# A hybrid recurrent, attention and expert layer: merging the branches with an accumulating DMA

## The chip, the cores and the metric

The kernel runs on one core of a Trainium2 chip. The core has five engines with queues of their own: TensorE (PE in the profile; PEld is its weight load), VectorE (DVE), ScalarE (ACT), GpSimd (POOL) and SyncE (SP). Each works through its instructions in order and waits where an instruction's input or buffer is not there. DMA transfers are issued from SP's queue or from GpSimd's. The metric is the time of one execution on the device, in microseconds (us); lower is better.

## The reference, cut to what matters

One layer over 1024 latent tokens of 1024 channels, with 256 context tokens ahead of them. A recurrent branch (`rnn`) and an attention branch (`attn`) are computed, merged with two sigmoid gates, projected, and added to the input; then a routed mixture of 16 experts follows. The change lies in the merge:

```python
def merge_branches(rnn, attn, zg, p):
    g = jax.nn.sigmoid(zg).reshape(B, L, N_BRANCH, D_MODEL)
    merged = g[:, :, 0] * (rnn @ p['w_rnn_out']) + g[:, :, 1] * (attn @ p['w_mla_out'])
    return merged @ p['w_o']

x_new = x + mod_l[2] * merge_branches(rnn_l, attn_l, z_l[5], p)
x_new = x_new + mod_l[5] * ec_moe(modulate(rmsnorm(x_new, p['g_norm2']), mod_l[3], mod_l[4]), p)
```

The experts can only begin when every token has been routed, and routing needs `x_new` of all tokens.

## The kernel before

All matrix products are made from pairs of values: `split` (lines 93 to 95) makes a high part by a cast on ACT and a low part by a subtraction on DVE, and `mm3` (lines 97 to 100) adds three products. The stages run one after the other: projections, recurrent branch, its output projection, attention, merge and output projection, routing, experts.

The first summand of the merge is finished early. Lines 858 to 869 multiply the recurrent branch's product by its gate and store it to `s0_d` in DRAM, as 8 blocks of 128 channels by 1024 tokens. The second gate lies in `s1_d` in the same form.

The merge is the stage opened at line 1007. It has two halves of 512 tokens (`hf`), each with 8 blocks of 128 channels (`b`). `mo_mm(hf, b)` makes the product of the attention branch with `w_mla_out`, 12 matmuls into one of three PSUM banks. `mo_out(hf, b)` (lines 1034 to 1042) loads `a0` (the finished first summand) and `s1` (the second gate), 256 KB each, from SP's queue; multiplies the product in PSUM by `s1` on DVE (line 1040), which frees the bank; adds `a0` on DVE (line 1041); and splits the sum into `mh` and `ml`. When the 8 blocks of a half are issued, `xo(ph, t)` multiplies them by `w_o`: 4 token tiles by two column halves, 24 matmuls each, which read `mh` and `ml` block by block (`k`) and pairs of split weights `woh`, `wol` (`load_wo`). In the first half the first three blocks are run over three quarters of the contraction before the last quarter, since the attention's last normalisation (lines 931 to 935: DVE, GpSimd, ACT, DVE for each of 8 slices) is still under way.

The order of the matmuls is written out by hand (`manual_schedule` over PE). On the other engines, and on SP's queue, a planner puts the instructions in order before the run from its own costs, so an instruction can stand ahead of one that the program names earlier; on the chip each queue then keeps that order. A tile of which `bufs` copies exist can be written again when the readers of the copy from `bufs` turns ago are done; both `a0` and `s1` have four copies.

Of the kernel before, what the change touches and what calls it, by code (L numbers as in the profile page):

```python
# [19 lines left out]
F32 = mybir.dt.float32  # L20
# [4 lines left out]
OP = mybir.AluOpType  # L25
AX = mybir.AxisListType

P = 128
D = 1024
KD = D // P  # L30
# [30 lines left out]
def layer_kernel(ctx: ExitStack, tc: tile.TileContext, I, rope_tab, out, dbg=None):  # L61
    nc = tc.nc
# [30 lines left out]
    def split(h, l, src):  # L93
        nc.scalar.copy(h, src)  # L94
        nc.vector.tensor_tensor(l, src, h.bitcast(F32), OP.subtract)  # L95
# [26 lines left out]
    s0_d = dram.tile([KD, P, SEQ], F32, name="s0_d")  # L122
# [771 lines left out]
    p6a = p6ac.__enter__()  # L894
# [114 lines left out]
    with pool("p6b", side="right") as p6b, pool("p6", side="right") as p6:  # L1009
# [11 lines left out]
        mw, mp, wo = {}, {}, {}  # L1021
# [11 lines left out]

        def mo_out(hf, b):
            ts = slice(hf * 512, (hf + 1) * 512)
            a0 = p6a.tile([P, 512], F32, name="a0", bufs=4)
            nc.sync.dma_start(a0, s0_d[b][:, ts])
            s1 = p6a.tile([P, 512], F32, name="s1", bufs=4)
            nc.sync.dma_start(s1, s1_d[b][:, ts])
            nc.vector.tensor_tensor(s1, mp.pop((hf, b)), s1, OP.mult)  # L1040
            nc.vector.tensor_tensor(s1, s1, a0, OP.add)
            split(mh[:, b], ml[:, b], s1)

        wraw = {}
# [84 lines left out]
        with tc.manual_schedule(engines={mybir.EngineType.PE}):  # L1129
            for hf in range(2):  # L1130
                if hf == 0:
                    for ks in (range(3), range(3, 4)):
                        for b in range(3):
                            mo_mm(0, b, ks)
                            if ks[0]:
                                mo_out(0, b)
# [3 lines left out]
                    for b in range(3, KD):  # L1140
                        mo_mm(0, b)
                        mo_out(0, b)
                        if b >= 4:
                            load_wo(0, b - 4)
                    nc.vector.scalar_tensor_tensor(bc[2], bc[2], 1.0, g2b, op0=OP.add, op1=OP.mult)
                else:
                    mh, ml = merged()
                    for b in range(KD):
                        mo_mm(1, b)
                        if b < 2:  # L1150
                            tail[0][b]()
                            if b == 1:
                                tail.pop()
                        mo_out(1, b)
# [213 lines left out]
```

## Time and profile before

| | us |
|---|---|
| median of 3 executions (lowest, highest) | 1769.93 (1767.58, 1776.2) |
| the profiled execution, its own time | 1771.81 |
| its span in the trace | 1769.8 |
| PE busy | 1687.1 (95%) |
| DVE busy | 1313.4 (74%) |
| ACT busy | 1014.9 (57%) |
| POOL busy | 264.5 (15%) |
| first half's blocks of the merge, first to last `mo` matmul | 988.75 to 1016.81 |
| second half's blocks | 1073.39 to 1096.52 |

A timeline row gives the start, the duration, the engine, the line, the operation, the tile written and the tiles read; in brackets stands how long the engine had been idle and what released it. Matmuls overlap, so a row of 0.39 us can be followed by the next 0.23 us later. In these views the digits of a tile's name are left out: `a` is `a0` and `s` is `s1` in the merge stage.

### The profile page before, as it was taken

Reading aid. Unit: us, or ns where it says so; the run is one execution under the profiler, and the core shown is the slowest. Engines: PE = TensorE matmul, PEld = TensorE weight load, DVE = VectorE, ACT = ScalarE, POOL = GpSimd, SP = SyncE. Lnnn points to the kernel's source line nnn. Section 1 sums busy time; section 2 is a strip of 40 time slices with the busy share of each in tenths; the row PEclk is TensorE's granted clock in tenths of the full one; section 3 lists DMA queues with packets and bytes.
Section 4 is the critical chain, followed back from the end, with each engine's and each line's share of the span. In section 5 each row is a group of like instructions: output and inputs, shape, how many; then the busy total and the mean of one; then the engine's idle time right before and its main releaser. Section 6 shows DMA issues by size and latency. Waiting matters only on the chain.

```text
span 1769.8 us, 20838 instructions
## 1 busy us (share of the span) xinstructions
PE 1687.1 (95%) x7823; PEld 1356.9 (77%) x7823; DVE 1313.4 (74%) x1607; ACT 1014.9 (57%) x1105; POOL 264.5 (15%) x196
## 2 busy tenths in 40 slices
PE   8999999999999999999999999939999999999996
PEld 3788887888887877777777678827888888888885
DVE  4755456788886454787877657587999999989996
ACT  2533324876788313667776532316777777777773
POOL 1123331211221100111210100020121111112101
PEclk9999999999999999999999999969999999999999
DMA  8264444435443934000000355667999999999981
GB/s 328 100 181 101 108 121 140 131 126 167 155 144 117 318 136 152 28 28 28 29 1 1 138 199 213 234 261 286 379 395 391 403 399 381 399 402 380 389 309 24
DMA packets 174179, 363.72 MB, mean 206 GB/s; under 512 B 40160, under 2 KB 90744, under 8 KB 174080
## 3 DMA queue, kind: packets, MB, share of 16 engines
q1 hardware_dynamic: 168896, 343.54, 53.6%
q0 software_dynamic: 5184, 18.88, 4.0%
q8 instruction: 61, 1.00, 0.2%
q14 instruction: 38, 0.31, 0.0%
HBM read 314.84 MB, written 47.54 MB: 205 GB/s over the span
## 4 chain that ended last, share of the span: by engine, by line
PE 71%; DVE 11%; ACT 6%; issue 4%; DMA 4%; POOL 3%; SPq 0%; POOLq 0%; DVEq 0%; ACTq 0%
PE w_e_gate L99 3%; PE w_e_gate L100 3%; PE w_e_gate L98 3%; PE w_e_down L99 3%; PE w_e_down L100 3%; PE w_e_down L98 3%; PE w_e_up L99 3%; PE w_e_up L98 3%; PE w_e_up L100 3%; PE z L99 2%; PE z L98 2%; PE z L100 2%; PE pm L816 2%; POOL st L143 2%; PE s L98 2%
## 5 line engine op out<-in xcount | busy, mean ns | idle before, releaser
L95 DVE TENSOR_TENSOR el<-ma,eh 128x2048 fp32r<-128x2048 f32 x114 | 258.2, 2286 | 22.2 <-PE w_e_down L99 10.8
L94 ACT CAST eh<-ma 128x2048 fp32r<-128x2048 f32 x114 | 217.9, 1917 | 73.7 <-PE w_e_up L100 28.7
L95 DVE TENSOR_TENSOR el<-me,eh 128x2048 fp32r<-128x2048 f32 x78 | 176.9, 2287 | 16.6 <-ACT eh L94 6.0
L94 ACT CAST eh<-me 128x2048 fp32r<-128x2048 f32 x78 | 149.0, 1916 | 47.4 <-PE w_e_gate L100 17.3
L906 ACT ACTIVATE pr<-s 128x512 f32<-128x512 f32 x160 | 95.8, 599 | 77.2 <-PE s L100 75.8
L818 DVE TENSOR_REDUCE mx<-pm 128x1 f32<-128x320 f32 x256 | 114.4, 483 | 22.8 <-PE pm L816 20.6
L99 PE MATMUL z<-xl,wh 128*128 128x512 f32 x320 | 125.2, 392 | 1.9 <-DVE xl L280 1.9
L98 PE MATMUL z<-xh,wh 128*128 128x512 f32 x320 | 125.2, 393 | 1.0 <-DVE xh L279 0.8
L100 PE MATMUL z<-xh,wl 128*128 128x512 f32 x320 | 125.0, 391 | 1.2 <-POOL wl L326 1.2
L1312 POOL DMA_INDIRECT out_dram<-y,icol x16 | 52.3, 3268 | 469.9 <-DVE y L1311 469.9
L94 ACT CAST wh<-wr 128x1024 fp32r<-128x1024 f32 (+1 forms) x53 | 52.0, 980 | 116.1 <-PE z L99 55.0
L95 DVE TENSOR_TENSOR pl<-pr,ph 128x1024 fp32r<-128x1024 f32 x64 | 81.0, 1265 | 31.4 <-ACT ph L94 24.7
L99 PE MATMUL w_e_up<-el,xgh 128*128 128x512 f32 x256 | 100.7, 394 | 0.6 <-DVE el L95 0.6
L98 PE MATMUL w_e_gate<-eh,xgh 128*128 128x512 f32 x256 | 101.1, 395 | 0.2 <-ACT xgh L94 0.2
L99 PE MATMUL w_e_gate<-el,xgh 128*128 128x512 f32 x256 | 101.2, 395 | 0.0
L100 PE MATMUL w_e_gate<-eh,xgl 128*128 128x512 f32 x256 | 100.1, 391 | 0.8 <-DVE xgl L95 0.8
L98 PE MATMUL w_e_down<-eh,hdh 128*128 128x512 f32 x256 | 99.7, 389 | 1.1 <-ACT hdh L94 1.1
L98 PE MATMUL w_e_up<-eh,xgh 128*128 128x512 f32 x256 | 100.7, 393 | 0.0
L99 PE MATMUL w_e_down<-el,hdh 128*128 128x512 f32 x256 | 100.6, 393 | 0.0
L100 PE MATMUL w_e_down<-eh,hdl 128*128 128x512 f32 x256 | 99.9, 390 | 0.5 <-DVE hdl L95 0.5
L100 PE MATMUL w_e_up<-eh,xgl 128*128 128x512 f32 x256 | 99.8, 390 | 0.0
L816 PE MATMUL pm<-kh,qh 97*128 97x320 f32 x256 | 86.6, 353 | 7.0 <-DVE kl L95 4.1
(349 smaller groups left out, 4368.7 us busy)
## 6 DMA issues: line engine op xcount, KB each, us to landing
ma<-in_w_e_down_dram SPq DMA_DIRECT2D x40, 1024.0 KB, 9.4
ma<-in_w_e_up_dram SPq DMA_DIRECT2D x38, 1024.0 KB, 8.0
ma<-in_w_e_gate_dram SPq DMA_DIRECT2D x36, 1024.0 KB, 7.2
me<-in_w_e_gate_dram SPq DMA_DIRECT2D x28, 1024.0 KB, 7.0
me<-in_w_e_up_dram SPq DMA_DIRECT2D x26, 1024.0 KB, 8.2
me<-in_w_e_down_dram SPq DMA_DIRECT2D x24, 1024.0 KB, 9.8
wr<-in_w_in_dram SPq DMA_DIRECT2D x32, 512.0 KB, 4.5
wr<-in_w_ada_dram SPq DMA_DIRECT2D x32, 512.0 KB, 4.2
```

Source lines behind the costliest of these rows:

```text
L94: nc.scalar.copy(h, src)
L95: nc.vector.tensor_tensor(l, src, h.bitcast(F32), OP.subtract)
L98: nc.tensor.matmul(o, lh, rh, start=start, stop=False)
L99: nc.tensor.matmul(o, lh, rl, start=False, stop=False)
L100: nc.tensor.matmul(o, ll, rh, start=False, stop=stop)
L143: nc.gpsimd.tensor_tensor(ap, ap, h, OP.pow)
L816: nc.tensor.matmul(pm[:, 0:320], qh[:, t * P:(t + 1) * P], kh[:, g * 320:(g + 1) * 320], start=True, stop=True)
L818: nc.vector.tensor_reduce(mx[:, g, t:t + 1], pm[:, 0:320], axis=AX.X, op=OP.max)
L906: nc.scalar.activation(pr[:, sl], sp_, AF.Exp)
L1312: nc.gpsimd.indirect_dma_start(out=out_rows, out_offset=bass.IndirectOffsetOnAxis(ap=icol[:, e:e + 1], axis=0), in_=y, in_offset=None, com ...
```

## The change

In blocks 0 to 5 of a half the addition on DVE goes. `s1` holds the gated attention product, and a DMA issued from GpSimd reads the first summand from DRAM and adds it into `s1` in place. The split of such a block is put into the program two blocks later (`late`). Blocks 6 and 7 keep the load of `a0` and the addition; ahead of block 6's multiplication the program splits what is still waiting (blocks 4 and 5). `s1` has six copies instead of four and `a0` two instead of four.

```diff
         def mo_out(hf, b):
             ts = slice(hf * 512, (hf + 1) * 512)
-            a0 = p6a.tile([P, 512], F32, name="a0", bufs=4)
-            nc.sync.dma_start(a0, s0_d[b][:, ts])
-            s1 = p6a.tile([P, 512], F32, name="s1", bufs=4)
+            s1 = p6a.tile([P, 512], F32, name="s1", bufs=6)
             nc.sync.dma_start(s1, s1_d[b][:, ts])
-            nc.vector.tensor_tensor(s1, mp.pop((hf, b)), s1, OP.mult)
-            nc.vector.tensor_tensor(s1, s1, a0, OP.add)
+            if b < KD - 2:
+
+                nc.vector.tensor_tensor(s1, mp.pop((hf, b)), s1, OP.mult)
+                nc.gpsimd.dma_start(out=s1, in_=s0_d[b][:, ts], accum_op=OP.add)
+                late.append((b, s1))
+            else:
+                a0 = p6a.tile([P, 512], F32, name="a0", bufs=2)
+                nc.sync.dma_start(a0, s0_d[b][:, ts])
+                while late:
+                    mo_split(*late.pop(0))
+                nc.vector.tensor_tensor(s1, mp.pop((hf, b)), s1, OP.mult)
+                nc.vector.tensor_tensor(s1, s1, a0, OP.add)
+                mo_split(b, s1)
+            if len(late) > 2:
+                mo_split(*late.pop(0))
+
+        late = []
+
+        def mo_split(b, s1):
             split(mh[:, b], ml[:, b], s1)
```

## Rows read from the trace of the kernel before

**Rows 1.** Page, part 4: the chain that ended last, shares by engine

```profile
PE 71%; DVE 11%; ACT 6%; issue 4%; DMA 4%; POOL 3%; SPq 0%; POOLq 0%; DVEq 0%; ACTq 0%
```

**Rows 2.** By stretches: length, busy PE, PEld, DVE, ACT, POOL, granted clock, DMA share, GB/s

```profile
997.00:1017.00 20.00, 16.86 (x61) 13.31 (x61) 17.41 (x26) 6.80 (x11) 1.51 (x1) 0.83 0.81 292
...
1001.00:1005.60 4.60, 4.60 (x12) 3.54 (x12) 3.98 (x7) 0.97 (x2) 0.00 (x0) 0.50 0.88 327
...
1073.00:1101.00 28.00, 28.00 (x132) 23.33 (x132) 21.55 (x40) 7.92 (x16) 0.55 (x1) 1.00 0.58 197
```

**Rows 3.** Timeline of PE in the first half of the merge stage

```profile
996.68 0.39 PE L100 MATMUL mo<-ath,wl 128*128 128x512 f32 x1
...
1000.15 0.80 PE L98 MATMUL mo<-ath,wh 128*128 128x512 f32 x1 [3.08 <-DVE s L1040]
...
1005.87 0.49 PE L99 MATMUL mo<-atl,wh 128*128 128x512 f32 x1
...
1017.04 0.39 PE L98 MATMUL xo<-woh,mh 128*128 128x512 f32 x1
...
1022.99 0.50 PE L99 MATMUL xo<-wol,mh 128*128 128x512 f32 x1 [1.28 <-DVE wol L95]
...
1024.97 0.50 PE L100 MATMUL xo<-woh,ml 128*128 128x512 f32 x1
```

**Rows 4.** Timeline of DVE, first half of the merge stage

```profile
997.32 1.21 DVE L95 TENSOR_TENSOR wol<-wr,woh 128x1024 fp32r<-128x1024 f32 x1
...
999.42 0.68 DVE L1040 TENSOR_TENSOR s<-mo,s 128x512 f32<-128x512 f32 x1
...
1013.45 0.68 DVE L1040 TENSOR_TENSOR s<-mo,s 128x512 f32<-128x512 f32 x1
...
1017.58 1.28 DVE L1041 TENSOR_TENSOR s<-s,a 128x512 f32<-128x512 f32 x2
...
1021.12 0.68 DVE L1040 TENSOR_TENSOR s<-mo,s 128x512 f32<-128x512 f32 x1
...
1021.73 1.21 DVE L95 TENSOR_TENSOR wol<-wr,woh 128x1024 fp32r<-128x1024 f32 x1
```

**Rows 5.** Timelines of DVE and PE, second half of the merge stage

```profile
1091.97 0.68 DVE L1040 TENSOR_TENSOR s<-mo,s 128x512 f32<-128x512 f32 x1
...
1096.75 0.39 PE L98 MATMUL xo<-woh,mh 128*128 128x512 f32 x1
...
1097.38 0.68 DVE L1040 TENSOR_TENSOR s<-mo,s 128x512 f32<-128x512 f32 x1
...
1099.48 0.69 DVE L95 TENSOR_TENSOR ml<-s,mh 128x512 fp32r<-128x512 f32 x1 [0.69 <-ACT mh L94]
...
1101.96 0.39 PE L100 MATMUL xo<-woh,ml 128*128 128x512 f32 x1
```

**Rows 6.** Instructions of tile mh: smallest, median, largest ns; first and last start

```profile
L94 ACT CAST mh<-s x16: 614/620/626, 1002.0 to 1098.8; 128x512 fp32r<-128x512 f32 x16
```

**Rows 7.** DMA issues: tiles, queue, count, KB, median us from issue to landing

```profile
s<-s_d SPq DMA_DIRECT2D x4, 256.0 KB, 3.8
...
xg<-h_d,icol POOLq DMA_INDIRECT x2, 4.5
...
rn_d<-ge POOLq DMA_DIRECT2D x1, 512.0 KB, 3.0
...
s_d<-sg POOLq DMA_DIRECT2D x3, 512.0 KB, 6.1
...
out_dram<-y,icol POOLq DMA_INDIRECT x16, 11.6
```

**Rows 8.** GpSimd beside VectorE: two timeline rows, and line 934 (smallest, median, largest ns)

```profile
577.53 3.49 DVE L95 TENSOR_TENSOR rl<-wr,rh 128x1024 fp32r<-128x1024 f32 x3
...
578.49 0.53 POOL L619 DMA_DIRECT2D s_d<-sg  x1
...
L934 POOL TENSOR_TENSOR num<-num,den x32: 448/462/1507, 765.5 to 997.3; 128x128 f32<-128x128 f32 x32
```

## The prediction

> **What bounds the kernel now.** I read the profile from the outside in: the chain of waits, then the merge stage by stretches, then that stage's timelines engine by engine, and last the DMA issues. The chain is 71% TensorE and 11% VectorE [rows 1], so time is won only where TensorE waits or runs slowly. In the stretch 997 to 1017 us, which holds most of the first half's blocks, DVE is busy 17.41 us of 20.00 and the granted clock averages 0.83; in the second half's stretch TensorE is busy 28.00 us of 28.00 and DVE 21.55 [rows 2]. So the reader is to see two halves with different limits.
>
> In the first half TensorE loses time in two places. After the 996.68 matmul it stands until 1000.15, because the three product banks are full until the first multiplication frees one; the cadence would have given 996.91, so 3.24 us go [rows 3]. Then it runs at the lower of its two clock levels (granted 0.50, 1.2 GHz) [rows 2]: 13 matmuls take 1000.15 to 1005.87, 5.72 us, where the full clock's cadence gives 13 x 0.2265 = 2.94; 2.78 us go. The cadence is that of the second half's first output tile, whose 24 matmuls start from 1096.75 to 1101.96, 23 steps in 5.21 us [rows 5]. The second place is the first half's first output tile: it starts at 1017.04 and its last matmul at 1024.97, where 5.21 us would give 1022.25 [rows 3]. That is 2.72 us, lost to DVE: the wait at 1022.99 is for a `w_o` split that DVE only began at 1021.73, right behind the last block's multiplication at 1021.12 [rows 3, 4]. The second half's first output tile has no such loss [rows 5].
>
> **The change part by part.** Twelve additions go, six in each half. A pair of them takes 1.28 us and a single such operation 0.68, so each costs the queue 0.60 us: 3.6 us of DVE per half [rows 4]. In the second half nothing waits for them: the last low part ends at 1099.48 + 0.69 = 1100.17, and the matmul that reads it first starts at 1101.96, a margin of 1.79 us [rows 5]. That part is worth nothing there.
>
> In the first half they stand in the queue that ends late. Two things move. First, `s1` of blocks 4 and 5 now has a copy of its own and is loaded ahead of the stage, and so is the `a0` of blocks 6 and 7. Block 4's multiplication ran at 1013.45 [rows 4]. In the second half the last multiplication started 0.63 us after the first output matmul (1097.38 against 1096.75) [rows 5]; put back by three blocks of 12 x 0.2265 = 2.72 us from 1017.04, block 4's could run at 1017.04 + 0.63 - 8.16 = 1009.5, block 5's at 1012.2, 6's at 1015.0, 7's at 1017.7. Second, what DVE still has to do from block 5's multiplication on: three multiplications, two additions and four splits, 9 x 0.60 = 5.4 us, and four operations on 1024 columns (three weight splits and one gain), each some 1.15 us of queue (1.21 less an overlap of about 0.06, an estimate from the 1.28 pair [rows 4]), 4.6 us. From 1012.2 that ends at 1022.2 if DVE never stands, and 1022.25 is what TensorE needs. I grant it 1 us of standing, about what the wait of 0.69 for a cast would make once or twice [rows 5]. So the first output tile loses about 1.0 us instead of 2.72: **a gain of 1.7 us**.
>
> What is added: twelve accumulating DMAs of 256 KB from GpSimd. No such DMA into SBUF is in the trace, so its time L from issue to landing is bounded by neighbours: a plain load of the same 256 KB lands in 3.8 us in this very stretch, plain stores of 512 KB from GpSimd's queue in 3.0 and 6.1, a gather of 512 KB into SBUF in 4.5, and the only accumulating ones, 512 KB scatters in the saturated expert stage, in 11.6 [rows 7]. I take L = 4.5, the row nearest in queue and direction, at twice the size, which makes up for the addition; the ends 3.0 and 11.6 stay for the range.
>
> The new wait is the cast `mh` on ACT, which now waits for a landing instead of a DVE addition; the weight casts queue behind it on ACT, and the low part and all later DVE work behind that cast. The cover is the delay of two blocks, 5.44 us. A block's multiplication (0.68), hand-over (0.1, estimate), landing (4.5) and cast (0.62 [rows 6]) take 5.9 us, so the low part comes just behind the multiplication two blocks on, and that one can be up to two blocks late before a bank is missed. Blocks 0 to 3 therefore cost nothing, even with L some 4 us longer. ACT, busy 6.80 us of 20.00, and GpSimd, 1.51 of 20.00 [rows 2], have room for waits and for twelve issues of about 0.53 us [rows 8]. On SP's queue twelve loads go. The load of block 6's `s1` now waits for block 0's split: 999.42 + 0.68 + 0.1 + 4.5 + 0.62 + 0.68 = 1006.0; with 3.8 to land it is there by 1009.8, and it is needed at 1015.0 (L = 11.6 would make it 2 us late).
>
> Block 5 is where the latency can show. First half: its multiplication ends at 1012.9, its sum lands at 1017.5, is cast by 1018.1, and its first reader, 15 steps into the output tile, is at 1020.4: covered. Second half: it ends at 1091.97 + 0.68 = 1092.65, the sum lands at 1097.25, is cast by 1097.9 and split by 1098.6; needed at 1096.75 + 15 x 0.2265 = 1100.15: covered. But in program order blocks 6 and 7 come behind that split: two multiplications, two additions and two splits from 1098.6, 6 x 0.60 = 3.6 us, the last low part done at 1102.3 where 1101.96 is needed, 0.4 us late; with the planner's order putting block 6 ahead, nothing. **I take a loss of 0.2 us.**
>
> One rule weighed. The trace has GpSimd's product of line 934 at 0.46 us in the median and 1.51 at the worst, and the worst is the one at 997.3, beside a DVE split of two SBUF operands [rows 4, 8]. But an issue from GpSimd's queue in the middle of three such splits took 0.53 us [rows 8]. The Trainium skill, page "SBUF — State Buffer", section "Who interferes with whom", says that a VectorE instruction with two SBUF inputs holds up a GpSimd instruction that reads SBUF, and only infers that descriptor generation is spared. The 0.53 us bears out the inference. By the rule without it each issue would take some 1.05 us more, and L would be 5.55: the second half's loss becomes about 1.2, and the gain of the whole falls to some 0.5 us.
>
> **The sum.** 1.7 - 0.2 = 1.5 us less. The profiled execution took 1771.81 us, 2.0 of it outside its span of 1769.8, and would take 1770.3; it lies 1.9 above the median of the three, so for the median I forecast 1769.93 - 1.5 = **1768.4 us**.
>
> **The rivals.**
> *Latency shows (slower).* The place is block 5 at the end of each half. The point is L = about 6: from there each further us costs both halves, some 2 us in all. At L = 8 block 5's cast in the second half ends at 1101.4, 1.25 us late, and the six DVE operations behind it leave the last low part about 2 us later still: 3.2 us there, and 3.2 instead of 2.72 in the first half, together 3.7 slower, 1773.6. At 11.6 both halves stop for about 4.9 us and trail 2 more, 6.9 + 6.9 - 2.7 = 11.1, and each stop, longer than the 3.24 us after which the clock fell [rows 2, 3], would bring the 2.78 us of slow matmuls again: 16.6 slower, 1786.5. For it: the only accumulating rows land in 11.6. Against: those scatters move twice the bytes, in a stage where expert weights fill the DMA engines; here the DMA share is 0.81 and 0.58 [rows 2].
>
> *The first stop goes too (faster).* If the planner's new order puts the first multiplication ahead of the `w_o` split at 997.32 and the normalisation's last piece, the 3.24 and 2.78 us go as well, and with all of the 2.72: 8.7 us, 1761.2. For it: that multiplication's product is complete by about 995, yet it ran at 999.42 [rows 4]. Against: what stands ahead of it is not touched by the change.
>
> *No effect.* The planner leaves the late `w_o` split where it is, the freed DVE time is idle, and the time stays at 1769.9. For it: the wait at 1022.99 is for that split, not for a sum [rows 3].
>
> **How the numbers follow.** Chances: forecast 0.52, with a range of its own of 1766 to 1771.5; no effect 0.12; latency 0.24, half of it beyond 8.85 us; first stop gone 0.12, two thirds of it, with some noise, beyond 8.85 us. A measurement of this kernel tells about 0.5%, 8.85 us, from no change. Faster by more than that: 0.08; slower: 0.12; within: 0.80. The range 1761 to 1779 leaves out half of the latency case and a little of the fastest.
>
> **What would show it.** Right: no additions on DVE for blocks 0 to 5; block 4's multiplication near 1009.5; accumulating DMAs landing in 3.8 to 6 us; the first half's first output tile spread over about 6 us instead of 7.9, the second's over 5.2 to 5.6. Wrong: a TensorE wait released by `mh` of block 5 in either half, a second stretch at clock 0.50, GpSimd issues far above 0.53 us, or a first multiplication that is not near 999.4.

## The result and the profile after

The changed kernel is slower: 1785.24 us in the median of 7 executions (1781.04 to 1847.76) against 1770.62 for the kernel before, timed beside it (1765.62 to 1776.2). The ratio is 1.0081 with a 95% interval of 1.0064 to 1.0098. The 1847.76 is the one slow execution, at a mean granted clock of 0.875 against 0.974 to 0.979 in the others, and the ratio leaves it out. The forecast was 1768.4 and its range ended at 1779. The two profiled spans are 1783.4 and 1769.8 us, 13.6 apart, and below that difference is taken apart.

The chain of the kernel after (page, part 4) has less TensorE and more waiting than before [rows 1]: TensorE falls from 71% to 65%, while DVE, ACT, DMA and issue gain 2, 1, 2 and 2 points.

```profile
PE 65%; DVE 13%; ACT 7%; DMA 6%; issue 6%; POOL 3%; SPq 0%; POOLq 0%; DVEq 0%; ACTq 0%
```

Next, the kernel after by stretches, with the columns of [rows 2]:

```profile
997.00:1017.00 20.00, 16.05 (x69) 12.97 (x70) 12.39 (x16) 5.73 (x8) 5.26 (x6) 1.00 0.97 282
...
1022.70:1029.00 6.30, 4.80 (x9) 2.51 (x9) 5.66 (x8) 2.59 (x4) 0.00 (x0) 0.59 0.92 345
...
1073.00:1101.00 28.00, 28.00 (x136) 23.34 (x135) 15.96 (x31) 6.75 (x17) 5.66 (x8) 1.00 0.64 180
1101.00:1125.00 24.00, 20.17 (x82) 15.06 (x81) 9.65 (x16) 6.84 (x11) 0.62 (x1) 0.86 0.77 258
...
1108.60:1116.30 7.70, 6.82 (x16) 4.56 (x17) 4.80 (x8) 2.30 (x5) 0.00 (x0) 0.58 0.48 166
```

DVE did become freer: 12.39 us of 20.00 instead of 17.41, and 15.96 of 28.00 instead of 21.55 [rows 2]. Yet there are two new stretches with a granted clock below 0.6, each right behind a stop of TensorE, and where the second half's blocks end TensorE is busy only 20.17 us of 24.00.

Where the 13.6 us lie (first starts of matmuls in the two traces; "first output tile" is the 24 matmuls that take 5.21 us without a stop):

| part | before | after | difference |
|---|---|---|---|
| start of span to first `mo` matmul | 988.75 | 986.91 | -1.84 |
| from there to the end of the first half's first output tile | 36.22 | 43.08 | +6.86 |
| of that, the tile itself | 7.93 | 14.97 | +7.04 |
| to the first `mo` matmul of the second half | 48.42 | 48.44 | 0.02 |
| second half's blocks | 23.36 | 23.36 | 0 |
| second half's first output tile | 5.21 | 11.13 | +5.92 |
| to its last output matmul | 47.25 | 49.03 | +1.78 |
| to the end of the span | 620.60 | 621.48 | +0.88 |

The first row lies ahead of the change; it is 984 to 989 in all the kernels below. Within the last, the experts take 570.2 before and 572.1 after, and 572.1 also in a kernel below whose time equals that of before. The 1.78 us ahead of it are matmuls that still run at the lower clock: nine steps take 3.79 us from 1112.92 to 1116.71, where the cadence gives 2.04. So some 14.6 us belong to the merge, and they lie where the blocks end and the first output tile reads them, in both halves.

TensorE of the kernel after in the first half (timeline; beside [rows 3]):

```profile
998.31 0.50 PE L98 MATMUL mo<-ath,wh 128*128 128x512 f32 x1 [3.07 <-DVE s L1040]
...
1012.12 0.51 PE L98 MATMUL mo<-ath,wh 128*128 128x512 f32 x1 [2.64 <-DVE s L1040]
...
1015.02 0.39 PE L98 MATMUL xo<-woh,mh 128*128 128x512 f32 x1
...
1022.67 0.79 PE L98 MATMUL xo<-woh,mh 128*128 128x512 f32 x1 [4.77 <-ACT woh L94]
...
1029.26 0.50 PE L98 MATMUL xo<-woh,mh 128*128 128x512 f32 x1 [0.75 <-ACT mh L94]
...
1029.99 0.51 PE L100 MATMUL xo<-woh,ml 128*128 128x512 f32 x1
```

The first stop, for a bank, is the old one. A second one for a bank is new (1012.12), and so is one of 4.77 us in the output tile. The matmul behind it reads block 4's `mh` and weights `woh`, and the cast of the weights came last. Next stand rows of GpSimd, ACT and DVE at these places (timelines; the last row of ACT is that cast):

```profile
1000.44 1.77 POOL L1041 DMA_DIRECT2D s<-s_d  x2 [0.95 <-DVE s L1040]
...
1007.88 0.62 ACT L94 CAST mh<-s 128x512 fp32r<-128x512 f32 x1 [5.69 <-DMA s<-s_d]
1010.13 0.62 ACT L94 CAST mh<-s 128x512 fp32r<-128x512 f32 x1 [1.63 <-DMA s<-s_d]
...
1021.06 0.62 ACT L94 CAST mh<-s 128x512 fp32r<-128x512 f32 x1 [6.81 <-DMA s<-s_d]
1021.58 1.04 ACT L94 CAST woh<-wr 128x1024 fp32r<-128x1024 f32 x1
...
1001.78 0.69 DVE L1040 TENSOR_TENSOR s<-mo,s 128x512 f32<-128x512 f32 x1
...
1008.53 0.69 DVE L95 TENSOR_TENSOR ml<-s,mh 128x512 fp32r<-128x512 f32 x1 [4.93 <-ACT mh L94]
...
1011.39 0.68 DVE L1040 TENSOR_TENSOR s<-mo,s 128x512 f32<-128x512 f32 x1
...
1021.71 0.69 DVE L95 TENSOR_TENSOR ml<-s,mh 128x512 fp32r<-128x512 f32 x1 [4.83 <-ACT mh L94]
1022.32 0.68 DVE L1048 TENSOR_TENSOR s<-mo,s 128x512 f32<-128x512 f32 x1
```

The reader is to see one cause in two queues. ACT stands 6.81 us for a landing before block 4's `mh`, and the cast `woh`, which needs no sum, stands behind it. `mh` is there at 1021.68 and `woh` at 1022.62: most of TensorE's 4.77 us is the late sum of block 4 itself, and the last 0.94 us are ACT's order. DVE stands 4.93 us for block 0's `mh` and 4.83 for block 4's. Behind the first of these waits come the low parts of blocks 0 and 1 and then block 4's multiplication, which is the program's own order: the multiplication runs at 1011.39, and TensorE has no bank until 1012.12.

The second half's TensorE, then DVE, then GpSimd and ACT (timelines; beside [rows 5]):

```profile
1101.79 0.39 PE L98 MATMUL xo<-woh,mh 128*128 128x512 f32 x1
...
1105.15 0.50 PE L100 MATMUL xo<-woh,ml 128*128 128x512 f32 x1
1108.60 0.50 PE L98 MATMUL xo<-woh,mh 128*128 128x512 f32 x1 [2.95 <-ACT mh L94]
...
1111.91 0.79 PE L98 MATMUL xo<-woh,mh 128*128 128x512 f32 x1 [0.88 <-ACT mh L94]
...
1089.65 0.69 DVE L95 TENSOR_TENSOR ml<-s,mh 128x512 fp32r<-128x512 f32 x1 [2.68 <-ACT mh L94]
...
1090.34 0.68 DVE L1040 TENSOR_TENSOR s<-mo,s 128x512 f32<-128x512 f32 x1
...
1097.24 0.69 DVE L95 TENSOR_TENSOR ml<-s,mh 128x512 fp32r<-128x512 f32 x1 [4.42 <-ACT mh L94]
1097.85 0.68 DVE L1040 TENSOR_TENSOR s<-mo,s 128x512 f32<-128x512 f32 x1
...
1104.40 0.69 DVE L95 TENSOR_TENSOR ml<-s,mh 128x512 fp32r<-128x512 f32 x1 [4.17 <-ACT mh L94]
1105.01 0.68 DVE L1048 TENSOR_TENSOR s<-mo,s 128x512 f32<-128x512 f32 x1
...
1091.54 0.86 POOL L1041 DMA_DIRECT2D s<-s_d  x1 [4.75 <-ACT mh L94]
...
1100.76 0.86 POOL L1041 DMA_DIRECT2D s<-s_d  x1 [0.84 <-DVE s L1040]
...
1096.59 0.62 ACT L94 CAST mh<-s 128x512 fp32r<-128x512 f32 x1 [5.09 <-DMA s<-s_d]
...
1107.93 1.14 ACT L94 CAST mh<-s 128x512 fp32r<-128x512 f32 x2 [3.56 <-DMA s<-s_d]
```

Here the loop can be read off. Block 2's multiplication starts at 1090.34 and ends at 1091.02; GpSimd begins the issue at 1091.54; the sum has landed when ACT casts at 1096.59; DVE makes the low part at 1097.24; and only then, at 1097.85, block 4's multiplication, because in this half the planner put the low part of block b ahead of the multiplication of block b+2 (of block 4, ahead of block 6, the program itself does). From 1090.34 to 1097.85 are 7.51 us for two blocks (0.68 multiplication, 0.52 hand-over, 5.05 landing, 0.65 cast, 0.61 low part). TensorE needs 24 x 0.2265 = 5.44 us for two. DVE falls 2 us behind at each pair; three banks hide this until the blocks end, and then block 5's `mh` stops TensorE for 2.95 us and block 7's for 0.88, with the lower clock behind. Of the 2.95 us some 2.2 are block 5's own landing: from its issue at 1100.76 it took 7.2 us, where the other five of this half took 4.7 to 5.3, and two loads of 1 MB each were issued from SP's queue from 1101.98 on.

The DMAs of the kernel after (the row of line 1041, then the time from issue to landing over both halves, then the DMA issues of 996 to 1033 and of 1073 to 1115; beside [rows 7, 8]):

```profile
L1041 POOL DMA_DIRECT2D s<-s_d x12: 854/862/1181, 998.6 to 1100.8; - x12
...
DMA to landing us min/median/max: 4.7/7.9/10.3
...
s<-s_d POOLq DMA_DIRECT2D x6, 256.0 KB, 9.5
...
s<-s_d POOLq DMA_DIRECT2D x6, 256.0 KB, 5.0
```

### The profile page after: what moved, and what is told of

Its sections match the earlier page's. It is cut to its first block, busy times and chain, and to the rows that moved or that the text cites. A ratio compares the mean times of both kernels' runs of the same rounds, so it can differ in the third digit from the quotient of the medians.

```text
span 1783.4 us, 20838 instructions
## 1 busy us (share of the span) xinstructions
PE 1692.6 (95%) x7823; PEld 1360.6 (76%) x7823; DVE 1308.7 (73%) x1595; ACT 1014.5 (57%) x1105; POOL 273.9 (15%) x208
## 4 chain that ended last, share of the span: by engine, by line
PE 65%; DVE 13%; ACT 7%; DMA 6%; issue 6%; POOL 3%; SPq 0%; POOLq 0%; DVEq 0%; ACTq 0%
PE w_e_gate L99 3%; PE w_e_gate L100 3%; PE w_e_gate L98 3%; PE w_e_down L99 3%; PE w_e_down L100 3%; PE w_e_down L98 3%; PE w_e_up L99 3%; PE w_e_up L98 3%; PE w_e_up L100 3%; PE pm L816 2%; DMA s<-s_d 2%; PE z L99 2%; POOL st L143 2%; PE z L100 2%; PE z L98 2%
## 5 line engine op out<-in xcount | busy, mean ns | idle before, releaser
L95 DVE TENSOR_TENSOR el<-me,eh 128x2048 fp32r<-128x2048 f32 x78 | 176.9, 2288 | 16.6 <-ACT eh L94 5.9
```

## The experiments

After the result my theory was: the low part waits on an in-order queue for a landing, and what stands behind it (multiplications on DVE, weight casts on ACT) is what TensorE misses. The rivals were the planner's new order by itself, the buffers, and the accumulation as opposed to a late fetch. All measured numbers in one table; the kernels follow. "To tile end" runs from the first `mo` matmul to the last matmul of the first half's first output tile; landings are medians of the two halves.

| kernel | ratio to before [95%] | to tile end | second half's tile | landings |
|---|---|---|---|---|
| before | 1 | 36.22 | 5.21 | |
| after | 1.0081 [1.0064, 1.0098] | 43.08 | 11.13 | 9.5, 5.0 |
| DVE adds, late split | 1.0003 [0.9992, 1.0014] | 36.22 | 5.21 | |
| buffers alone | 1.0001 [0.9989, 1.0013] | 36.96 | 5.21 | |
| GpSimd adds | 1.0055 [1.0037, 1.0073] | 38.19 | 8.60 | |
| after, program order | 1.0141 [1.0119, 1.0163] | 49.84 | 12.75 | 8.9, 5.3 |
| before, program order | 1.0078 [1.0058, 1.0097] | 44.80 | 7.27 | |
| four blocks, not six | 1.0057 [1.0038, 1.0076] | 39.23 | 7.37 | 9.6, 5.1 |
| broadcasts later | 1.0071 [1.0051, 1.0091] | 42.06 | 8.97 | 7.3, 5.2 |
| plain load, late | 1.0077 [1.0057, 1.0097] | 42.04 | 6.81 | 6.0, 3.8 |
| splits three blocks late | 1.0058 [1.0043, 1.0073] | 41.25 | 6.97 | 8.0, 7.3 |
| first half alone | 1.0044 [1.0032, 1.0057] | 43.47 | 5.21 | 8.9 |
| second half alone | 1.0037 [1.002, 1.0055] | 35.13 | 10.81 | 5.1 |

**DVE adds, late split.** The change without its DMA:

```diff
             if b < KD - 2:
-
+                a0 = p6a.tile([P, 512], F32, name="a0", bufs=2)
+                nc.sync.dma_start(a0, s0_d[b][:, ts])
                 nc.vector.tensor_tensor(s1, mp.pop((hf, b)), s1, OP.mult)
-                nc.gpsimd.dma_start(out=s1, in_=s0_d[b][:, ts], accum_op=OP.add)
+                nc.vector.tensor_tensor(s1, s1, a0, OP.add)
                 late.append((b, s1))
```

> The additions of blocks 0 to 5 are back on DVE with a0 loaded from SP's queue; the buffers (six s1, two a0) and the split two blocks later stay as in the changed kernel. Theory (the landing of the accumulating DMA is what costs): within 0.25% of the kernel before (ratio 0.9975 to 1.0025), the second half's first output tile in 5.2 to 5.8 us instead of the changed kernel's 11.1, no cast waiting for a DMA. Rival (the later split and the reordered queues cost by themselves): ratio above 1.005 and a second tile of 8 us or more.

The time is that of before. Late splits, six copies of `s1` and two of `a0` cost nothing; the loss comes with the DMA in the addition's place. Nor is it the planner's order by itself: here too, in the second half, a low part stands ahead of a later multiplication (block 4's at 1091.92, block 5's multiplication at 1092.53), and the tile takes 5.21 us.

**Buffers alone.** The kernel before with six copies of `s1` and two of `a0`:

```diff
-            a0 = p6a.tile([P, 512], F32, name="a0", bufs=4)
+            a0 = p6a.tile([P, 512], F32, name="a0", bufs=2)
...
-            s1 = p6a.tile([P, 512], F32, name="s1", bufs=4)
+            s1 = p6a.tile([P, 512], F32, name="s1", bufs=6)
```

> The kernel before with six copies of s1 and two of a0 and nothing else. Theory: the loads of the gate for blocks 4 and 5 come earlier, the first half's first output tile loses some 1 us less: ratio 0.998 to 1.001. Rival (the buffers and SP's queue behind them are what costs): ratio above 1.004, with loads of w_o landing later than before.

The first half's blocks end 25.16 us after their first matmul (28.29 before), but the first output tile then takes 11.80 instead of 7.93, and its end comes at 36.96 instead of 36.22. While DVE does the additions, the first half ends with DVE's queue, and TensorE's head start is given back in the tile.

**GpSimd adds.** `a0` is loaded ahead and added by GpSimd:

```diff
             if b < KD - 2:
-
+                a0 = p6a.tile([P, 512], F32, name="a0", bufs=2)
+                nc.sync.dma_start(a0, s0_d[b][:, ts])
                 nc.vector.tensor_tensor(s1, mp.pop((hf, b)), s1, OP.mult)
-                nc.gpsimd.dma_start(out=s1, in_=s0_d[b][:, ts], accum_op=OP.add)
+                nc.gpsimd.tensor_tensor(s1, s1, a0, OP.add)
```

> As the changed kernel, but the sum of blocks 0 to 5 is made by an addition on GpSimd from a0 loaded ahead, in place of the accumulating DMA; VectorE is relieved of the same six additions, and the planner's order on DVE again has low parts ahead of later multiplications. Theory (latency): an addition takes 1.2 to 2.5 us instead of the 5.0 and 9.5 us of a landing, so the second tile is 5.2 to 6 us and the ratio to the kernel before 0.996 to 1.002. Rival (the planner's order costs, whatever the latency): second tile 8 us or more, ratio above 1.004.

Here the rival's case came: with no landing behind the multiplication two thirds of the loss remain. (In the first half GpSimd still waits for landings, those of `a0`, which now has two copies: 5.44 us before its addition at 1009.84.) DVE and GpSimd in the second half, then DVE beside a GpSimd addition in the first (timelines):

```profile
1093.86 0.68 DVE L1041 TENSOR_TENSOR s<-mo,s 128x512 f32<-128x512 f32 x1
1096.65 0.69 DVE L95 TENSOR_TENSOR ml<-s,mh 128x512 fp32r<-128x512 f32 x1 [2.11 <-ACT mh L94]
1097.26 0.68 DVE L1041 TENSOR_TENSOR s<-mo,s 128x512 f32<-128x512 f32 x1
...
1094.67 1.29 POOL L1042 TENSOR_TENSOR s<-s,a 128x512 f32<-128x512 f32 x1 [2.11 <-DVE s L1041]
...
1003.18 2.31 DVE L95 TENSOR_TENSOR wl<-wr,wh 128x1024 fp32r<-128x1024 f32 x1
...
1002.64 1.77 POOL L1042 TENSOR_TENSOR s<-s,a 128x512 f32<-128x512 f32 x1 [1.67 <-DMA a<-s_d]
```

In this kernel the order is strict: multiplication, GpSimd addition, cast, low part of the same block, next multiplication, 1093.86 to 1097.26 = 3.40 us per block, against TensorE's 2.72. So in the second half it is not the landing as such that costs, but any wait between two multiplications that makes a block longer than TensorE's. Beside a GpSimd addition a weight split takes 2.31 us instead of 1.21. The Trainium skill, page "SBUF — State Buffer", section "Who interferes with whom", has this rule: a VectorE instruction with two SBUF inputs contends with a GpSimd instruction that reads SBUF. The two rows agree with it.

**Program order.** Two kernels: the changed one with DVE and ACT in the order of the program in the blocks of both halves, and the kernel before with the same edit.

```diff
                 if hf == 0:
...
+                    with tc.manual_schedule(engines={mybir.EngineType.PE, mybir.EngineType.DVE, mybir.EngineType.Activation}):
+                        for ks in (range(3), range(3, 4)):
...
+                    with tc.manual_schedule(engines={mybir.EngineType.PE, mybir.EngineType.DVE, mybir.EngineType.Activation}):
+                        for b in range(KD):
```

> The changed kernel with DVE and ACT held to the program's order within the blocks of both halves, so that the multiplication two blocks on stands ahead of a block's low part. Theory, if latency costs by way of the order in the queues: in the second half landings stay near 5 us but multiplications run when their product is done, and the first output tile falls from 11.1 us to 5.5 to 7; in the first half little is won, since the w_o splits now stand behind the late sums; ratio to the kernel before 1.002 to 1.008. Rival (the landing of block 5 alone is too late, whatever the order): second tile 9 us or more, ratio 1.007 or more.

My theory missed: the kernel became slower still, and the rival's numbers came (second tile 12.75 us, ratio 1.0141). In the first half program order put `w_o`'s casts behind the `mh` casts on ACT, and TensorE stood 10.70 us until one of them, begun at 1025.38, was done; the `mh` of the same matmul was there at 1019.70. In the second half it put the routing of the last tokens of the first half ahead of block 1's multiplication on DVE, which ran at 1093.64, 8.0 us after block 0's. So this run has losses that the changed kernel hasn't, and doesn't tell what the planner's order alone costs.

> The kernel before, with VectorE and ScalarE in program order within the blocks of both halves, and no DMA that adds. It tells how much of the loss of the changed kernel in program order (ratio 1.0141) is the order and how much the landings. Theory (the order alone costs only the first half, where the w_o splits come behind the blocks; no operation waits for a landing that adds): second half's first output tile 5.2 to 6 us, first half's 8 to 12, the time 0 to 5 us above the kernel before, a ratio of 1.000 to 1.003. Rival (program order itself is what costs): second tile above 8 us, a ratio of 1.008 or more.

Neither expectation held: the ratio is nearly the rival's 1.008, the second half's tile between the two. In its second half, too, block 1's multiplication comes 8.0 us after block 0's (1092.60 and 1084.61), behind the routing. DVE of this kernel in the first half (timeline):

```profile
1001.25 0.68 DVE L1040 TENSOR_TENSOR s<-mo,s 128x512 f32<-128x512 f32 x1
1001.97 0.69 DVE L1041 TENSOR_TENSOR s<-s,a 128x512 f32<-128x512 f32 x1
1003.35 0.69 DVE L95 TENSOR_TENSOR ml<-s,mh 128x512 fp32r<-128x512 f32 x1 [0.69 <-ACT mh L94]
1003.95 0.68 DVE L1040 TENSOR_TENSOR s<-mo,s 128x512 f32<-128x512 f32 x1
```

One block takes 1001.25 to 1003.95 = 2.70 us of DVE's queue, 0.69 of it standing for the cast, so each weight split of 1.2 us makes it late. The planner's order, which can fill that wait with other work, is worth 0.78% to the kernel before. Of the 1.41% that the changed kernel loses in program order, 0.63 points are left to the DMAs and the late splits.

**Four blocks, not six.** Blocks 4 and 5 keep `a0` and the addition, so the last landing comes two blocks earlier:

```diff
-            if b < KD - 2:
+            if b < KD - 4:
```

> The changed kernel with accumulating DMAs for blocks 0 to 3 of a half only; blocks 4 to 7 load a0 and add on DVE. Theory (a late landing holds DVE up, and what counts is how much of the half is left to catch up): the second half's first output tile falls from 11.1 us to 5.5 to 8, the first half's from 15.0 to 8 to 11; ratio to the kernel before 1.001 to 1.006. Rival (only the issue and the transfer themselves cost, each DMA the same): two thirds of the changed kernel's loss stay, ratio near 1.0055 with a second tile of 9 us.

The two output tiles shrink to 8.50 and 7.37 us, as the theory said. The ratio doesn't tell the two apart, since 1.0057 lies in the theory's range and at the rival's 1.0055; and the profiled execution, 1776.23 us, is the fastest of four with a median of 1781.61, so its trace shows less than the whole loss. The wait for a bank stays, at 1011.39, now 3.69 us, for block 4's multiplication, ahead of which this program names the splits of blocks 2 and 3. So the losses in the tiles belong mostly to blocks 4 and 5, and four landings a half, those of blocks 0 to 3, still cost 0.57% alone.

**Broadcasts later.** The three `bc` loads and that of `g2b`, 2 MB, are named after the last block instead of before block 3:

```diff
-                    for m in range(3):
-                        nc.sync.dma_start(bc[m], bcast(mod_d[m], D))
-                    nc.sync.dma_start(g2b, bcast(I["g_norm2"], D))
                     for b in range(3, KD):
...
                             load_wo(0, b - 4)
+                    for m in range(3):
+                        nc.sync.dma_start(bc[m], bcast(mod_d[m], D))
+                    nc.sync.dma_start(g2b, bcast(I["g_norm2"], D))
```

> The changed kernel with the four broadcast loads of 512 KB (three of the modulation rows and the norm's gain) named after the first half's last block instead of after its third. Theory (bulk loads in flight share the DMA engines and stretch the landing): the first half's first four accumulating DMAs land in 4.5 to 6.5 us instead of 9 to 10, and block 4's multiplication no longer makes TensorE wait 2.6 us for a bank; the last two land late as before, the first output tile stays above 10 us, ratio to the kernel before 1.004 to 1.009. Rival (an accumulating DMA of 256 KB takes 9 us by itself in this half): landings unchanged.

SP issued the four loads at 997.24, 1002.36, 1008.25 and 1008.73, where in the kernel after they follow each other from 997.25 to 998.74; so they are spread out and not gone. The first half's landings fall from 9.5 to 7.3 us and the wait for a bank at 1012 is gone, so the bulk loads do lengthen landings; of the first four only two (4.6 and 6.0) lie in the expected 4.5 to 6.5, the others take 7.4 and 7.2. The tile still takes 14.04 us (14.97), and the ratio falls only within its interval. Its stop is nearly as long as that of the kernel after, and here a sum ends it, block 5's (timeline of TensorE):

```profile
1022.95 0.79 PE L98 MATMUL xo<-woh,mh 128*128 128x512 f32 x1 [4.46 <-ACT mh L94]
```

**Plain load, late.** GpSimd loads the first summand into the gate's buffer after the multiplication, without adding; DVE adds just ahead of the late split (in `mo_split`). `r1` has three copies, `s1` four and `a0` one:

```diff
-            s1 = p6a.tile([P, 512], F32, name="s1", bufs=6)
+            s1 = p6a.tile([P, 512], F32, name="s1", bufs=4)
...
-                nc.vector.tensor_tensor(s1, mp.pop((hf, b)), s1, OP.mult)
-                nc.gpsimd.dma_start(out=s1, in_=s0_d[b][:, ts], accum_op=OP.add)
-                late.append((b, s1))
+                r1 = p6a.tile([P, 512], F32, name="r1", bufs=3)
+                nc.vector.tensor_tensor(r1, mp.pop((hf, b)), s1, OP.mult)
+                nc.gpsimd.dma_start(out=s1, in_=s0_d[b][:, ts])
+                late.append((b, r1, s1))
...
-                a0 = p6a.tile([P, 512], F32, name="a0", bufs=2)
+                a0 = p6a.tile([P, 512], F32, name="a0", bufs=1)
```

> In blocks 0 to 5 the multiplication writes a tile of its own, and GpSimd then issues a plain load of the first summand into the gate's buffer, which the multiplication has just read; the addition is on DVE, with the split, two blocks later. So the same 256 KB come from the same queue at the same point without the addition in the DMA. Theory (reading and writing the destination is a part of the landing): the loads land in the second half in 3 to 4 us instead of 5.0 and the ratio is 1.002 to 1.007. Rival (it is GpSimd's queue and the sharing of the engines): 5.0 within 0.5 us, and as many DMA us per transfer as the accumulating ones (1.4 to 1.7 us of all 16 engines).

DMAs of this kernel: the row of line 1041, then queue 0 and the issues in 1073 to 1115.

```profile
L1041 POOL DMA_DIRECT2D s<-s_d x12: 536/538/594, 997.6 to 1098.5; - x12
...
q0 software_dynamic: 480, 1.57, 14.2%
...
s<-s_d POOLq DMA_DIRECT2D x6, 256.0 KB, 3.8
```

The same six DMAs of the kernel after, in the same stretch:

```profile
q0 software_dynamic: 864, 1.57, 23.9%
```

Accumulating makes the same bytes dearer: 0.86 us of issue instead of 0.54, 864 packets instead of 480, and 5.0 us instead of 3.8 to land (9.5 instead of 6.0 in the first half). The landing came as the theory said, the ratio, 1.0077, just above its 1.007. It is that of the kernel after within the intervals, with six DVE additions more per half and a second tile of 6.81 us. So there is a loss of this size without the adding too: both kernels fetch the summand only when the product is there, while the kernel before has it in SBUF by then.

**Splits three blocks late.** Program order, each split behind the multiplication and the issue of the block three later, `w_o`'s splits named one block earlier and ahead of the `mh` casts:

```diff
-                while late:
-                    mo_split(*late.pop(0))
...
-                mo_split(b, s1)
-            if len(late) > 2:
+                late.append((b, s1))
+            while late and (len(late) > 3 or b == KD - 1):
                 mo_split(*late.pop(0))
...
+                            if b < KD - 1:
+                                load_wo(0, b - 3)
                             mo_out(0, b)
```

> Accumulating DMAs as in the changed kernel; DVE and ACT in program order within the blocks, each split three blocks late and behind the multiplication (and, in blocks 6 and 7, the addition) of the newer block, and the w_o splits named ahead of the blocks' sums. Theory (order in the queues turns latency into lost time): the second half's first output tile takes 5.2 to 6.5 us with landings still near 5, no bank wait in the first half, whose first tile takes 8 to 11 us since landings there stay at 9; ratio to the kernel before 0.999 to 1.004. Rival (latency costs in any order): second tile above 8 us and ratio above 1.006.

The result lies between the two: a second tile of 6.97 us, and a ratio nearer to the rival's. No second wait for a bank and no wait for a weight cast remain, and from the first program-order kernel's 1.0141 it comes down to 1.0058. It does not reach the kernel before: the landings of the second half lengthen to 7.3 us, and the last splits are all made at the end of a half, where the output tile reads them.

**One half alone.** Two kernels, with `hf == 0` and with `hf == 1`:

```diff
-            if b < KD - 2:
+            if b < KD - 2 and hf == 0:
```

> The change in the first half of the merge alone; the second half keeps loads of a0 and additions on VectorE. Theory (each half loses by itself, because the low parts of the split wait on VectorE for landings and hold up the next multiplications): the first half's first output tile takes 12 to 15 us as in the changed kernel (14.97), the second half's 5.2 as before, GpSimd's six DMAs land in 9 to 10 us, and the time is some 5 to 8 us above the kernel before, a ratio of 1.003 to 1.0045. Rival (the loss is one effect of the whole stage, such as the buffers or traffic that the first half hands on): this run shows either nearly all of the 14.6 us, or none of it.

> The change in the second half of the merge alone. Theory: the first half runs as in the kernel before (first mo matmul to the end of its first output tile in 36 to 37 us), the second half's first output tile takes 10 to 12 us instead of 5.21 and a stretch at the lower clock level follows it, the DMAs land in about 5 us, and the time is some 6 to 9 us above the kernel before, a ratio of 1.0035 to 1.005; the two halves' losses add up to the 14.6 us of the change within 3 us. Rival (one effect of the whole stage): nearly all of the 14.6 us, or none.

Both ratios came as the theory said, and neither as the rival did: 0.44% and 0.37% add up to the change's 0.81%. Each half loses by itself, and the other keeps about its time of before (5.21, and 35.13, a little below the expected 36). The first half's tile, 15.27 us, and its landings, 8.9, are just outside what was expected. TensorE of the first kernel, first half, and of the second, second half (timelines):

```profile
1024.67 0.80 PE L98 MATMUL xo<-woh,mh 128*128 128x512 f32 x1 [4.76 <-ACT woh L94]
```

```profile
1102.85 0.50 PE L98 MATMUL xo<-woh,mh 128*128 128x512 f32 x1 [2.04 <-ACT mh L94]
1106.16 0.80 PE L98 MATMUL xo<-woh,mh 128*128 128x512 f32 x1 [0.74 <-ACT mh L94]
```

The stop of 4.76 us that ends with `woh` returns, and so do the stops for `mh` with the lower clock behind. No kernel here is faster than the one before.

## Why the prediction was wrong, step by step

**"Blocks 0 to 3 therefore cost nothing, even with L some 4 us longer."** This is the step that failed: with the DMAs of blocks 0 to 3 alone the kernel loses 0.57%. It took two blocks, 5.44 us, as cover, and two more before a bank is missed, which is room for L = 8.5, with "the low part ... just behind the multiplication two blocks on". In the first half the low parts of blocks 0 and 1 both stand ahead of block 4's multiplication, in the program too. From block 1's cast at 1010.13 to TensorE's next matmul at 1012.12 are 1.99 us, and the cadence wanted that matmul at 1009.32. So the DMA issued at 1000.44 had room for some 6.9 us, an estimate from these rows, and took 9.7. In the second half the planner put the low part just ahead of that multiplication, not behind. So the latency closes a loop through DVE's queue whose other parts take 2.46 us and which so has room for 5.44 - 2.46 = 2.98 us of landing: at L = 5.0 it takes 7.5 us per two blocks, 2 us lost per pair. That DVE's order is the planner's was known; the sum was made in program order all the same. Whether program order would have saved the second half stays open: the two kernels in that order lose 1.41% and, with splits three blocks late, 0.58%, but that order alone costs the kernel before 0.78%.

**The landing time L.** Taken as 4.5 with bounds of 3.0 and 11.6, measured 5.0 in the second half (4.7 to 7.2) and 9.5 in the first (8.7 to 10.3). The row nearest in queue and direction [rows 7] was good for the quiet half only. The DMA share of 0.81, which the prediction held against the latency rival, spoke for it: bulk loads lengthen a landing, as the kernel with the broadcasts later shows. In the Trainium skill, page "DMA: Bandwidth & Descriptors", section "Anatomy of one DMA — SWDGE (gpsimd) path", a fit gives 2.0 us and the bytes over 436 GB/s, for 256 KB an estimate of 2.6 us. No landing here is that short; the plain load's median in the quiet half is 3.8.

**ACT and GpSimd "have room".** Busy time was low, but room in an in-order queue is not had behind a wait. The prediction wrote that the weight casts queue behind `mh`, and then priced this at nothing; it is the last 0.94 us of TensorE's longest stop, 4.77 us. The rest is block 4's sum: its DMA, issued at 1012.36, took 8.7 us, and with 4.5 its `mh` would have been there at 1017.5, ahead of the 1017.74 that the cadence wanted. The issue takes 0.86 us and not 0.53 (inside L), and the hand-over before it 0.52 and not 0.1: 0.42 us more in each loop, nearly as much as the error of L in the second half. The rule on GpSimd beside VectorE, weighed there at 1.05 us more for each issue, did not show: the median of twelve is 0.862, and the issue at 1002.76, beside a weight split, took 0.854.

**The gain of 1.7 us.** DVE's 3.6 us per half were removed, as forecast. TensorE did not receive them: DVE stood for `mh` instead, 4.93 and 4.83 us at a time in the first half. The copies of their own for blocks 4 to 7 are worth nothing by themselves (ratio 1.0001), and block 4's multiplication ran at 1011.39, not at 1009.5, although the stage began 1.84 us earlier.

**The 2.78 us of slow matmuls.** They are not there after the first stop of the kernel after, though that stop is as long as before (3.07 and 3.08 us in brackets). Of the two kernels that equal the one before, the first shows a granted clock of 0.91 in the stretch 997 to 1017 and the second 1.00; so I don't credit it to the change.

**The rivals.** *Latency shows* named the mechanism and the end of the half where the first readers stop: block 5's `mh` in the second half, a second slow stretch, issues far above 0.53 us all came. Its threshold of L = 6 and its place were too narrow: the loop runs through all blocks, and the first half stops at block 4, for its sum and then for a weight cast. Its price at 11.6, 16.6 us, is near the 14.6 measured, but by luck, since it is made of other terms: the stops are 4.77 and 2.95 us, not 4.9 twice, and no landing took 11.6. *The first stop goes too* and *no effect* did not come. (The product that the former names was complete at 995.7, not by 995; nothing hangs on it.)

**Not settled.** Whether an accumulating DMA issued from another queue, or with the first summand kept in SBUF, would land soon enough was not tried. How much of the first half's loss is the longer landing is only bounded: with landings 2.2 us shorter its tile's end moves by 1.0 us. What the planner's order adds in the second half was not isolated, since the kernels in program order change more than that.

## What to carry to other kernels

An accumulating DMA can't be fetched ahead: what was a load hidden by four buffers becomes a latency behind the product, so put the measured landing (here 5 to 9.5 us for 256 KB, of which the issue takes 0.86) into the loop that frees the next buffer, and compare it with the time of the blocks that cover it. Look in the order that each queue really has for what stands behind the wait: a weight cast or a multiplication that needs nothing of the landing waits with it. Look also at which of a matmul's inputs came just before the last one: here the weight cast that ended the longest stop was only 0.94 us behind the sum. Freed busy time is a gain only if the queue isn't given a wait in its place.

## What had not been expected of the hardware

- An accumulating DMA of 256 KB from DRAM into SBUF makes 144 packets where a plain one makes 80 (864 and 480 for six), takes 0.86 us of GpSimd instead of 0.54, and lands 1.2 us later in the quieter half, 3.5 later in the busier one. The issue is as long with DVE idle (0.86 at 1093.33) as beside a DVE weight split (0.854 at 1002.76, the smallest), so it isn't contention with DVE.
- Beside a GpSimd addition a DVE split of 128x1024 took 2.31 us, 1.91 times its 1.21.
- TensorE stood 3.08 us in one kernel and ran at granted clock 0.50 behind it, and 3.07 us in another and did not; after stops of 4.77 and 2.95 us it did again (0.59 and 0.58).
